# The down projection of a two-layer decoder: from plain tiles to one level of Strassen with left factors kept in DRAM

## The chip, the cores and the metric

One core of one Trainium2 chip runs the whole program. The metric is device time in microseconds; each kernel is run several times and the median is taken. The engines are named as in the profile: PE (TensorE matmul), PEld (its weight load), DVE (VectorE), ACT (ScalarE), POOL (GpSimd), SP (SyncE, which here only issues DMAs).

## The reference

Two layers, sequence length S = 1024, model width D = 1024, all fp32. Each layer is a mixer block (four kinds of mixer side by side, then an output projection), a layer norm, a gated feed-forward part of width 2816, and a second layer norm:

```
for l in range(DEPTH):
    h = mixer_block(x, w_in[l], ...)
    x = layer_norm(ALPHA * x + h, ln1_g[l], ln1_b[l])
    f = swiglu(x, w_gate[l], w_up[l], w_down[l])
    x = layer_norm(ALPHA * x + f, ln2_g[l], ln2_b[l])

def swiglu(x, w_gate, w_up, w_down):
    g = jnp.einsum('bsd,df->bsf', x, w_gate)
    u = jnp.einsum('bsd,df->bsf', x, w_up)
    return jnp.einsum('bsf,fd->bsd', jax.nn.silu(g) * u, w_down)
```

## The kernel before, in words

Every large matmul runs in fp32r as three matmuls: an operand is split into a high part (ACT, `split` L234) and a low part (DVE, or POOL where asked, L235), and hi·hi, hi·lo and lo·hi are added in one PSUM bank.

The feed-forward part has two stages for each layer. **f1** (gate and up) walks over i = 0..21, 22 tiles of 128 hidden units. For each i it does one level of Strassen: seven products of 12 matmuls each, 128x512 wide (`prod`), 84 matmuls an i. The right factors B11, T1 and so on of each i are formed by DVE and split into a ring of 12 tiles `wb`; the left factors (A11, S1 and so on, of the layer's input) were split once and stay in `RA`. DVE adds the products up in pieces of the big fp32 tile `FA`; p1, sg, v and w of an i are such pieces, and two sets alternate (`f1_tmp(i % 2)`). `f1_out` leaves the hidden values of the first 512 tokens in v and of the other 512 in w, and POOL writes both to DRAM (`hid`, L1229 and L1230). The last i has its own order of products (`f1_last`).

**f2** (down) is a plain product: 22 tiles of hidden units by 8 tiles of 128 tokens by two halves of the output by three, 1056 matmuls of 128x512 a layer. It goes over the 22 tiles in three chunks (8, 8, 6). A chunk's weights are loaded whole (512 KB a tile) and split into `RA` or `wy`; for each token tile the hidden values come back from `hid` (L1283), are split into a tile `h` on ACT and DVE, and two banks are added to the token's x in `FA` (L1330). In the first chunk x comes from DRAM (L1308) and POOL multiplies and shifts it by ln1 (L1311, L1312). After the last chunk come the layer norm, and in the first layer the transposes for the next (`make_T`).

Each engine takes its instructions in one fixed order, set when the program is built; instructions inside `high_priority` are drawn forward by a number of places (`w_ahead`). DMAs are issued by SP for loads and mostly by POOL for stores.

SBUF is laid out by pools: `RA` (all fp32r data that live long) first, `FA` behind it, and behind that the tiles of the stage: `wx` and `e` of the output projection, `wb` of f1, `wy` and `h` of f2. `FA` has 12168 words in each partition, 48672 bytes, which is 95 x 512 + 32; all other tiles are multiples of 512 bytes. So in the kernel before every stage tile starts 32 bytes off the 512-byte grid on which `RA` stands.

Of the kernel before, what the change touches and what calls it, by code (L numbers as in the profile page):

```python
# [9 lines left out]
F32 = mybir.dt.float32  # L10
# [38 lines left out]
F_SIZE = C_G1 + 16  # L49
# [91 lines left out]
class Trunk:  # L141
    def __init__(self, tc, t, scr):
        self.tc, self.nc, self.t, self.scr = tc, tc.nc, t, scr
        self.wring = [0, 1, 2]
        self.wpos = 0
        self.rpos = 0
        self.mmp = 0
# [943 lines left out]
    def form(self, tt):  # L1091
# [6 lines left out]
              (self.xt(1), self.xt(5)), (self.xt(0), self.xt(4)))[p]  # L1098
# [28 lines left out]
        S1 = self.xt((4, 5, 2, 3)[p])[:, 0:512]  # L1127
# [33 lines left out]
    def f1_prep(self, l, i):  # L1161
# [3 lines left out]
        T1, T2, T3, T4 = (self.f(FX + 2048 + j * 512, 512) for j in range(4))  # L1165
# [58 lines left out]
    def f1_out(self, i):  # L1224
        nc = self.nc
        p1, sg, v, w = self.f1_tmp(i)
        nc.scalar.activation(w, w, AF.Silu)
        nc.vector.tensor_tensor(w, w, p1, ALU.mult)
        nc.gpsimd.dma_start(self.scr["h"][i, 0], v)  # L1229
        nc.gpsimd.dma_start(self.scr["h"][i, 1], w)  # L1230
        del self.blk[i]

    def f1_last(self, i):
# [8 lines left out]
        tt_(p1, w, bank, ALU.add)  # L1242
        bank = self.prod(i, "A11", "B11")
# [23 lines left out]

    def f2(self, l):
        nc, t = self.nc, self.t
        lng, lnb = self.LNP[:, 0:1024], self.LNP[:, 1024:2048]  # L1270
        last = len(CHUNKS) - 1
        bp = hp = 0

        def load_h(tt, f0, nf):
            nonlocal hp
            raw = self.f(F_RAW + (self.rpos % NRAW) * 1024, nf * 128)
            self.rpos += 1
            H = self.H[hp % 3]
            hp += 1
            hh, hl = H[:, 0:nf * 128], H[:, 1024:1024 + nf * 128]  # L1280
            with self.tc.high_priority(offset=self.w_ahead):
                src = self.scr["h"][f0:f0 + nf, tt // 4, :, (tt % 4) * 128:(tt % 4) * 128 + 128]
                nc.sync.dma_start(raw.rearrange("p (f n) -> p f n", f=nf), src.rearrange("f p n -> p f n"))  # L1283
                self.split(hh, hl, raw)
            return hh, hl

        for ci, (f0, nf) in enumerate(CHUNKS):
            self.wring, self.wpos = DOWN_SLOTS[ci], 0
            units = []
            pre = {}  # L1290
            for i in range(nf):
                units.append(self.wload(t["w_down"][l, f0 + i]))
                if ci == 0 and i < 3:
                    pre[i] = load_h(i, f0, nf)
            if ci != 1:
                g, b = (t["ln1_g"], t["ln1_b"]) if ci == 0 else (t["ln2_g"], t["ln2_b"])
                nc.sync.dma_start(lng, g[l].partition_broadcast(128))
                nc.sync.dma_start(lnb, b[l].partition_broadcast(128))
                if ci == 0:
                    self.copy(lng, lng, scale=ALPHA)  # L1300
                    self.copy(lnb, lnb, scale=ALPHA)
            groups = [(0, 1, 2)] + [(i,) for i in range(3, 8)] if ci == 0 else [(i,) for i in range(8)]
            for group in groups:
                hs = [pre[tt] if tt in pre else load_h(tt, f0, nf) for tt in group]
                if ci == 0:
                    with self.tc.high_priority(offset=self.w_ahead):
                        for tt in group:
                            nc.sync.dma_start(self.xt(tt), self.scr["x1"][tt * 128:(tt + 1) * 128, :])  # L1308
                    for tt in group:
                        x = self.xt(tt)  # L1310
                        nc.gpsimd.tensor_tensor(x, x, lng, ALU.mult)  # L1311
                        nc.gpsimd.tensor_tensor(x, x, lnb, ALU.add)  # L1312
                banks = [self.B[(0, 1, 2, 3, 6, 7)[(bp + i) % 6]] for i in range(2 * len(group))]
                bp += len(banks)
                order = [(i, (ch,)) for ch in range(2) for i in range(nf)] if ci == last and group == (7,) \
                    else [(i, (0, 1)) for i in range(nf)]
                for i, chs in order:
                    for q, (hh, hl) in enumerate(hs):
                        hi, lo = hh[:, i * 128:(i + 1) * 128], hl[:, i * 128:(i + 1) * 128]
                        for ch in chs:  # L1320
                            wh, wl = (w[:, ch * 512:(ch + 1) * 512] for w in units[i])
                            bank = banks[2 * q + ch]
                            self.mm(bank, hi, wh, i == 0, False)
                            self.mm(bank, hi, wl, False, False)
                            self.mm(bank, lo, wh, False, i == nf - 1)
                for q, tt in enumerate(group):
                    x = self.xt(tt)
                    for ch in range(2):
                        xc = x[:, ch * 512:(ch + 1) * 512]
                        nc.vector.tensor_tensor(xc, xc, banks[2 * q + ch], ALU.add)  # L1330
                    if ci == last:
                        if l == L - 1:
                            rows = t["out"][tt * 128:(tt + 1) * 128, :]
                            self.layer_norm(x, lng, lnb, lambda c, xc: nc.sync.dma_start(
                                rows[:, c * 512:(c + 1) * 512], xc))
                        else:
                            self.layer_norm(x, lng, lnb)
                            nc.gpsimd.dma_start(self.scr["x2"][tt * 128:(tt + 1) * 128, :], x)
                            self.make_T(tt, x)
# [109 lines left out]
    def run(self):  # L1449
# [3 lines left out]
        nc.vector.memset(self.f(C_MH, 1), -0.5)  # L1453
        for l in range(L):
# [12 lines left out]
            with tc.tile_pool(name=f"f2_{l}", bufs=1, reuse_waits="tile") as pool:  # L1467
# [4 lines left out]
def trunk_kernel(tc, t, ext=None):  # L1472
    with tc.tile_pool(name="sb", bufs=1) as pool, \
            tc.tile_pool(name="ps", bufs=1, space=bass.MemoryType.PSUM) as psum, \
# [5 lines left out]
            "h": dram.tile([NFT, 2, 128, 512], F32, name="hid"),  # L1480
# [7 lines left out]
        k.setup(pool, psum)  # L1488
# [98 lines left out]
```

## Time and profile before

| | before |
|---|---|
| median of 3 runs | 2600.79 us (2598.32 to 2601.14) |
| profiled execution, own time | 2604.73 us |
| its span, first to last instruction | 2603.0 us |
| mean granted TensorE clock | 0.987 |
| f1 of layer 1, of layer 2 | about 606 to 1053.9, about 1894 to 2342 us |
| f2 of layer 1, of layer 2 | 1053.7 to about 1308, 2342 to 2603 us |

The times in the profile are those of one execution, some 4 us above the median. The granted clock is a share of TensorE's full speed. "Idle before" an instruction is time in which its engine had nothing to run, put down to what released it.

### The profile page before, as it was taken

How to read it: one execution, taken by the hardware profiler on the slowest of the kernel's cores; microseconds unless marked ns; L12 is line 12 of the kernel's file. 1: busy time of each engine (PE TensorE's matmuls, PEld its weight loads, DVE VectorE, ACT ScalarE, POOL GpSimd, SP SyncE). 2: the span in 40 equal slices, each digit the busy share in tenths (PEclk: the TensorE clock that was granted, in tenths of full speed). 3: DMA queues.
4: the chain of work that ended last, by engine and by line, in shares of the span. 5: the costliest groups of instructions: out<-in, count | busy, mean ns of one | idle time of the engine just before them, and what ended most of it. 6: DMA issues, size and time to landing. Idle time of an engine off the chain costs nothing. (4 is left out here: it accounts for less than half of the span.)

```text
span 2603.0 us, 36989 instructions
## 1 busy us (share of the span) xinstructions
PE 2519.5 (97%) x14128; PEld 2110.5 (81%) x14128; DVE 1606.5 (62%) x3267; ACT 1004.7 (39%) x1934; POOL 489.2 (19%) x498
## 2 busy tenths in 40 slices
PE   8999998998999999999999999989989999999998
PEld 8988887786888888788899988877768888887886
DVE  4775356668766665632757753566797666656336
ACT  4776552235333332221246765521453333322110
POOL 2214131124000000700222231301230000007002
PEclk9999999998999999999999999999989999999999
DMA  4112123213222223532321120142222222235222
GB/s 159 51 39 71 35 64 114 90 50 110 98 80 85 74 81 100 168 119 69 118 76 53 48 65 28 62 137 66 81 97 97 76 81 87 73 106 191 83 85 77
DMA packets 120673, 224.24 MB, mean 86 GB/s; under 512 B 16816, under 2 KB 67888, under 8 KB 120496
## 3 DMA queue, kind: packets, MB, share of 16 engines
q1 hardware_dynamic: 107792, 179.93, 21.9%
q0 software_dynamic: 12704, 41.95, 4.3%
q8 instruction: 111, 1.82, 0.3%
q14 instruction: 66, 0.54, 0.1%
HBM read 167.77 MB, written 46.20 MB: 82 GB/s over the span
## 5 line engine op out<-in xcount | busy, mean ns | idle before, releaser
L222 PE MATMUL bank<-RA,wb 128*128 128x512 f32 x3600 | 846.0, 397 | 10.4 <-ACT wb L234 7.4
L222 PE MATMUL bank<-RA 128*128 128x256 f32 (+6 forms) x5016 | 819.7, 314 | 14.3 <-ACT XA L229 10.2
L222 PEld LDWEIGHTS bank<-RA,wb 128*128 128x128 f32 x3600 | 679.5, 189 | 176.8 <-ACT wb L234 8.3
L222 PEld LDWEIGHTS bank<-RA 128*128 128x128 f32 (+1 forms) x5016 | 691.6, 192 | 76.9 <-issue 22.6
L222 PE MATMUL bank<-RA,h 128*128 128x512 f32 x1728 | 412.8, 396 | 6.2 <-DVE RA L235 5.5
L222 PEld LDWEIGHTS bank<-RA,h 128*128 128x128 f32 x1728 | 323.3, 188 | 86.8 <-DVE RA L235 7.3
L234 ACT ACTIVATE wb<-FA 128x512 fp32r<-128x512 f32 x300 | 188.5, 633 | 499.5 <-PE bank L222 479.5
L235 DVE TENSOR_TENSOR wb<-FA,wb 128x512 fp32r<-128x512 f32 x300 | 208.3, 699 | 5.6 <-ACT wb L234 3.4
L256 POOL TENSOR_TENSOR RA<-FA,RA 128x512 fp32r<-128x512 f32 (+2 forms) x112 | 144.1, 1306 | 320.9 <-ACT RA L255 296.9
L522 ACT ACTIVATE XA<-XA,FA 128x128 f32<-128x128 f32 (+3 forms) x192 | 148.5, 774 | 44.7 <-DVE FA L517 42.8
L517 DVE CUSTOM_DVE_ANT_0 XA<-bank,XA 128x384 f32<-128x384 f32 (+2 forms) x192 | 109.6, 571 | 75.8 <-PE bank L222 73.9
L235 DVE TENSOR_TENSOR RA<-FA,RA 128x1024 fp32r<-128x1024 f32 (+2 forms) x64 | 94.4, 1491 | 95.1 <-ACT RA L234 94.1
L1229 POOL DMA_DIRECT2D hid<-FA x44 | 23.9, 542 | 671.5 <-DVE FA L1220 640.1
L1330 DVE TENSOR_TENSOR FA<-FA,bank 128x512 f32<-128x512 f32 x96 | 64.2, 684 | 133.2 <-PE bank L222 133.2
L234 ACT ACTIVATE RA<-FA 128x512 fp32r<-128x512 f32 (+2 forms) x96 | 78.3, 826 | 169.0 <-DMA FA<-in_w_down 119.4
L225 PE MATMUL bank<-FA,XA 128*128 128x128 f32 (+1 forms) x824 | 127.0, 275 | 8.8 <-DMA XA<-mixed 5.2
L229 ACT ACTIVATE XA<-bank 128x512 f32<-128x512 f32 (+5 forms) x228 | 104.0, 483 | 55.7 <-PE bank L225 43.7
L225 PEld LDWEIGHTS bank<-FA,XA 128*128 128x128 f32 (+1 forms) x824 | 97.5, 141 | 21.7 <-DMA XA<-mixed 5.9
L234 ACT ACTIVATE h<-FA 128x1024 fp32r<-128x1024 f32 (+1 forms) x48 | 46.7, 988 | 170.8 <-PE bank L222 142.2
L280 POOL TENSOR_SCALAR FA<-FA 128x1 f32<-128x1 f32 (+1 forms) x48 | 17.7, 368 | 505.3 <-DVE FA L984 350.7
L222 PE MATMUL bank<-XA 128*64 128x128 f32 (+1 forms) x836 | 93.9, 294 | 7.9 <-ACT XA L229 4.7
L222 PE MATMUL bank<-wx,RA 128*128 128x512 f32 x384 | 99.7, 412 | 0.0
(190 smaller groups left out, 2679.4 us busy)
## 6 DMA issues: line engine op xcount, KB each, us to landing
FA<-in_w_in SPq DMA_DIRECT2D x44, 512.0 KB, 3.6
FA<-in_w_gate SPq DMA_DIRECT2D x44, 512.0 KB, 3.6
FA<-in_w_up SPq DMA_DIRECT2D x44, 512.0 KB, 3.3
hid<-FA POOLq DMA_DIRECT2D x88, 256.0 KB, 2.3
FA<-in_w_down SPq DMA_DIRECT2D x44, 512.0 KB, 3.4
FA<-hid SPq DMA_DIRECT2D x32, 512.0 KB, 4.0
x<-FA POOLq DMA_DIRECT2D x24, 512.0 KB, 3.0
FA<-x SPq DMA_DIRECT2D x24, 512.0 KB, 4.0
```

Source lines behind the costliest of these rows:

```text
L222: self.nc.tensor.matmul(out, lhsT=lhsT, rhs=rhs, start=start, stop=stop)
L225: self.nc.tensor.transpose(out, src, self.FA[0:p, C_ID:C_ID + p])
L229: self.nc.scalar.activation(out, src, AF.Copy)
L234: self.nc.scalar.activation(hi, src, AF.Copy)
L235: (self.nc.gpsimd if pool else self.nc.vector).tensor_tensor(lo, src, hi.bitcast(F32), ALU.subtract)
L256: nc.gpsimd.tensor_tensor(lo[:, c], raw[:, c], hi[:, c].bitcast(F32), ALU.subtract)
L280: nc.gpsimd.tensor_scalar(out, var, EPS, 1.0, ALU.add, ALU.mult)
L517: nc.vector.tensor_tensor_reduce(sv[m][:, c0:c0 + wd], bank[:, 0:wd], mask[:, off:off + wd], -scale, init, ALU.add, ALU.min, acc)
L522: self.last_exp = nc.scalar.activation(sv[m][:, 0:n], sv[m][:, 0:n], AF.Exp, bias=nb[:, m:m + 1], scale=-1.0, accum_out=den[:, m:m + 1])
L1229: nc.gpsimd.dma_start(self.scr["h"][i, 0], v)
L1330: nc.vector.tensor_tensor(xc, xc, banks[2 * q + ch], ALU.add)
```

## The change

The down projection becomes one level of Strassen, as f1 already is. Output, hidden values and w_down are cut in two along each axis; seven phases (`DOWN`) each multiply one left factor by one right factor. A phase has four units (token tiles of 128 out of 512), a unit 11 steps j by three matmuls of 128x512 into one bank: 7 x 4 x 33 = 924 matmuls a layer where there were 1056. Each unit's bank is added by DVE to between one and four half rows of x.

- The left factors are made and split while f1 runs. After every second i (`f1_left`), POOL forms S1 to S4 by four additions. For each of the seven factors, `left_put` splits it into one of three tiles `st` (high part on ACT, low part on POOL), and POOL writes the tile, 512 KB, to DRAM in pieces of 1 KB. In f2 each unit loads its ready-made pair of parts, 1.44 MB in three pieces, into six tiles `h`.
- w_down is loaded in half-width blocks (256 KB) and stays raw in SBUF; DVE forms T1 to T4 in place; each phase splits 11 blocks (ACT high, DVE low).
- All loads of f2 are chained on SP in program order (`in_order`).
- The SBUF layout: `FA` goes to the right end, `RA` becomes `RB` and two tiles `RT` (which turn into raw weights `RW` in f2), and every fp32r tile now starts at the same place modulo 512 bytes.
- `f1_last` takes its products in another order, with A11 and A12 last.

The core of the diff:

```diff
@@ F_SIZE
-F_SIZE = C_G1 + 16
+F_SIZE = C_G1 + 16 + 80
+DOWN = [("A12", "B21"), ("S4", "B22"), ("A11", "B11"), ("S1", "T1"), ("S3", "T3"), ("S2", "T2"), ("A22", "T4")]
...
@@ f1_out
-        nc.gpsimd.dma_start(self.scr["h"][i, 0], v)
-        nc.gpsimd.dma_start(self.scr["h"][i, 1], w)
         del self.blk[i]
+        self.f1_left(i)
+
+    def left_put(self, j, name, src):
+        st = self.ST[self.lfp % 3].rearrange("p (t h n) -> p t h n", t=4, h=2)
+        self.lfp += 1
+        self.split(st[:, :, 0, :], st[:, :, 1, :], src.rearrange("p (t n) -> p t n", t=4), True)
+        self.nc.gpsimd.dma_start(self.scr["s" + name][:, :, j, :].rearrange("t p n -> p t n"),
+                                 st.rearrange("p t h n -> p t (h n)").bitcast(F32))
+
+    def f1_left(self, i):
+        tt_ = self.nc.gpsimd.tensor_tensor
...
+        if i % 2 == 0:
+            self.left_put(j, "A12", vb)
+            self.left_put(j, "A22", wb)
+            return
...
+        tt_(S1, wa, wb, ALU.add)
+        tt_(S2, S1, va, ALU.subtract)
+        tt_(S4, vb, S2, ALU.subtract)
+        tt_(S3, va, wa, ALU.subtract)
+        self.left_put(j, "A11", va)
+        self.left_put(j, "S4", S4)
+        self.left_put(j, "S1", S1)
+        self.left_put(j, "S3", S3)
+        self.left_put(j, "S2", S2)
...
@@ f2
+        self.in_order(nc.sync.dma_start(lng, t["ln1_g"][l].partition_broadcast(128)))
+        self.in_order(nc.sync.dma_start(lnb, t["ln1_b"][l].partition_broadcast(128)))
+        self.copy(lng, lng, scale=ALPHA)
+        self.copy(lnb, lnb, scale=ALPHA)
+        for j in range(NPR):
+            self.down_load(l, j, "B21")
+            self.down_put(0, j)
...
+                    self.mm(bank, hh, wh, j == 0, False)
+                    self.mm(bank, hh, wl, False, False)
+                    self.mm(bank, hl, wh, False, j == NPR - 1)
```

ACT at the passage from f1 to f2 in the first layer, before. `h` are the split hidden values of the first three token tiles, L1227 and L1249 the last activations of f1, `RA` the first down weights:

```order
L229 ACTIVATE FA_71<-bank1_73 128x512
L229 ACTIVATE FA_71<-bank4_76 128x512
L1249 ACTIVATE FA_71<-FA_71 128x512
L234 ACTIVATE h0_8292<-FA_71 128x1024
L234 ACTIVATE h1_8293<-FA_71 128x1024
L234 ACTIVATE h2_8294<-FA_71 128x1024
L1227 ACTIVATE FA_71<-FA_71 128x512
```

The same place now. L1254 and L1306 are the last activations of f1, the `st` rows are the high parts of A11, S1, S4, S3 and S2 of the last pair (in this order), L258 the scaling of ln1, and `RB` and behind it the first down weights:

```order
L1254 ACTIVATE FA_80<-FA_80 128x512
L1306 ACTIVATE FA_80<-FA_80 128x512
L261 ACTIVATE st0_5764<-FA_80 128x4x128
L261 ACTIVATE st2_5766<-FA_80 128x4x128
L261 ACTIVATE st1_5765<-FA_80 128x4x128
L261 ACTIVATE st0_5764<-FA_80 128x4x128
L261 ACTIVATE st1_5765<-FA_80 128x4x128
L258 ACTIVATE lnp0_8546<-lnp0_8546 128x1024
L258 ACTIVATE lnp1_8547<-lnp1_8547 128x1024
L261 ACTIVATE RB_79<-FA_80 128x512 x6
```

Before, the first splits of f2 stood ahead of the last activation of f1; now seven instructions stand between the last activation of f1 and the first split of f2, and the fourth and fifth of the five `st` rows write a tile that an earlier one of them filled.

POOL at the same place, before (L1229 and L1230 are the stores of hidden values, L1311 and L1312 x by ln1):

```order
L1230 DMA hid_66<-FA_71 128x512
L1229 DMA hid_66<-FA_71 128x512
L1311 TENSOR_TENSOR FA_71<-FA_71,LNP_8291 128x1024 x6
L1230 DMA hid_66<-FA_71 128x512
L1312 TENSOR_TENSOR FA_71<-FA_71,LNP_8291 128x1024 x2
L1311 TENSOR_TENSOR FA_71<-FA_71,LNP_8291 128x1024
```

And now: L1278, L1281, L1279 and L1280 are S1, S3, S2 and S4 of the last pair, L262 low parts, L1264 stores of left factors, L1372 and L1373 x by ln1:

```order
L1278 TENSOR_TENSOR FA_80<-FA_80 128x512
L1281 TENSOR_TENSOR FA_80<-FA_80 128x512
L1279 TENSOR_TENSOR FA_80<-FA_80 128x512
L262 TENSOR_TENSOR st0_5764<-FA_80,st0_5764 128x4x128
L262 TENSOR_TENSOR st2_5766<-FA_80,st2_5766 128x4x128
L1280 TENSOR_TENSOR FA_80<-FA_80 128x512
L1264 DMA leftA11_71<-st0_5764 128x4x256
L1264 DMA leftS1_72<-st2_5766 128x4x256
L262 TENSOR_TENSOR st1_5765<-FA_80,st1_5765 128x4x128
L1264 DMA leftS4_70<-st1_5765 128x4x256
L262 TENSOR_TENSOR st0_5764<-FA_80,st0_5764 128x4x128
L1264 DMA leftS3_73<-st0_5764 128x4x256
```

Before the x rows POOL now has four additions, five low parts and five stores of the last pair, and the stores of A11 and S4 stand behind S4's addition.

## Rows read from the trace of the kernel before

**Rows 1.** The page's part 1: engine, busy time, share of the span, instructions.

```profile
PE 2519.5 (97%) x14128; PEld 2110.5 (81%) x14128; DVE 1606.5 (62%) x3267; ACT 1004.7 (39%) x1934; POOL 489.2 (19%) x498
```

**Rows 2.** Groups of PE's instructions, shapes apart: busy, mean ns, idle before.

```profile
L222 PE MATMUL bank<-RA,wb 128*128 128x512 f32 x3600 | 846.0, 397 | 10.4 <-ACT wb L234 7.4 <-POOL RA L235 3.0
...
L222 PE MATMUL bank<-RA,h 128*128 128x512 f32 x1728 | 412.8, 396 | 6.2 <-DVE RA L235 5.5 <-DVE h L235 0.5
```

**Rows 3.** Busy time by window: PE, PEld, DVE, ACT, POOL, PEclk, DMA share, GB/s.

```profile
740.00:1040.00 300.00, 300.00 (x1288) 241.50 (x1287) 190.61 (x297) 93.43 (x150) 17.00 (x32) 1.00 0.25 84
1054.00:1062.00 8.00, 7.95 (x35) 6.11 (x34) 4.90 (x6) 3.82 (x4) 2.68 (x2) 1.00 0.89 339
...
0.00:20.00 20.00, 12.60 (x63) 11.52 (x64) 4.11 (x7) 6.83 (x11) 5.52 (x10) 1.00 0.86 305
590.00:630.00 40.00, 31.38 (x139) 24.52 (x137) 33.33 (x58) 25.21 (x46) 20.81 (x22) 0.90 0.18 71
```

**Rows 4.** Timeline of PE: start, length from first to last, one unbroken series each.

```profile
899.72 22.56 PE L222 MATMUL bank<-RA,wb 128*128 128x512 f32 x96
...
1236.76 5.76 PE L222 MATMUL bank<-RA,h 128*128 128x512 f32 x24
1242.36 2.91 PE L222 MATMUL bank<-wy,h 128*128 128x512 f32 x12
...
1689.24 16.41 PE L222 MATMUL bank<-RA 128*128 128x512 f32 x71
```

**Rows 5.** Timeline of the passage from f1 to f2 in layer 1.

```profile
1049.58 2.95 ACT L234 ACTIVATE h<-FA 128x1024 fp32r<-128x1024 f32 x3
...
1053.72 10.27 PE L222 MATMUL bank<-RA,h 128*128 128x512 f32 x42
...
1053.92 0.69 DVE L1252 TENSOR_TENSOR FA<-FA,bank 128x512 f32<-128x512 f32 x1 [1.32 <-PE bank L222]
...
1058.12 2.26 ACT L231 ACTIVATE LNP<-LNP 128x1024 f32<-128x1024 f32 x2 [2.85 <-DMA LNP<-in_ln_g]
...
1059.32 18.11 POOL L1311 TENSOR_TENSOR FA<-FA,LNP 128x1024 f32<-128x1024 f32 x6 [5.88 <-issue]
...
1061.71 16.79 DVE L235 TENSOR_TENSOR RA<-FA,RA 128x1024 fp32r<-128x1024 f32 x5 [3.10 <-ACT RA L234]
...
1065.22 8.43 PE L222 MATMUL bank<-RA,h 128*128 128x512 f32 x35 [1.23 <-DVE RA L235]
```

**Rows 6.** Single lines: durations in ns, least, median and most.

```profile
L235 POOL TENSOR_TENSOR RA<-FA,RA x32: 1282/1602/2800, 573.4 to 1922.1; 128x512 fp32r<-128x512 f32 x32
...
L1311 POOL TENSOR_TENSOR FA<-FA,LNP x16: 2389/3368/3398, 1059.3 to 2386.4; 128x1024 f32<-128x1024 f32 x16
...
L1071 POOL DMA_DIRECT2D x<-FA x16: 590/606/624, 567.0 to 1908.3; - x16
```

**Rows 7.** DMA issues: count, size each, median us from issue to landing.

```profile
hid<-FA POOLq DMA_DIRECT2D x88, 256.0 KB, 2.3
...
x<-FA POOLq DMA_DIRECT2D x24, 512.0 KB, 3.0
...
mixed<-FA POOLq DMA_DIRECT2D x2, 1024.0 KB, 12.7
```

**Rows 8.** Timeline of PE around its longest wait ahead of f1.

```profile
605.73 1.12 PE L225 MATMUL bank<-FA 128*128 128x128 f32 x4 [3.84 <-ACT FA L1070]
...
606.50 4.19 PE L222 MATMUL bank<-wx,RA 128*128 128x512 f32 x9
...
611.19 1.90 PE L222 MATMUL bank<-wx,RA 128*128 128x512 f32 x6
```

**Rows 9.** Timeline inside f1 (DVE and ACT while PE runs on).

```profile
908.14 0.63 ACT L234 ACTIVATE wb<-FA 128x512 fp32r<-128x512 f32 x1 [2.17 <-PE bank L222]
...
911.12 0.69 DVE L1217 TENSOR_TENSOR FA<-FA,bank 128x512 f32<-128x512 f32 x1 [1.51 <-PE bank L222]
911.72 0.68 DVE L1218 TENSOR_TENSOR FA<-FA,bank 128x512 f32<-128x512 f32 x1
```

More of the change, by code (lines that the diff above doesn't have):

```diff
@@ L178, in open_f1 @@
         self.WB = [pool.tile([128, 1024], F32R, name=f"wb{i}") for i in range(12)]
+        self.ST = [pool.tile([128, 1024], F32R, name=f"st{i}") for i in range(3)]
     def open_f2(self, pool):
-        self.WX = [pool.tile([128, 2048], F32R, name=f"wy{i}") for i in range(2)]
-        self.LNP = pool.tile([128, 2048], F32, name="LNP")
-        self.H = [pool.tile([128, 2048], F32R, name=f"h{i}") for i in range(3)]
+        tiles = {}
+        for name, dt in F2_TILES:
+            tiles[name] = pool.tile([128, 1024], dt, name=name)
+        self.DW = [tiles[f"dw{i}"] for i in range(4)]
+        self.H = [tiles[f"h{i}"] for i in range(6)]
+        self.LNP = [tiles[f"lnp{i}"] for i in range(2)]
+        self.WD = [tiles[f"wd{i}"] for i in range(3)]
     def r(self, off, n, p0=0, p1=128):
-        return self.RA[p0:p1, off:off + n]
+        if off >= R_W:
+            return self.RB[p0:p1, off - R_W:off - R_W + n]
+        return self.RT[off // 8192][p0:p1, off % 8192:off % 8192 + n]
     def f(self, off, n, p0=0, p1=128):
@@ L1265, in f1, with down_raw, in_order @@
                 self.f1_last(i)
+    def down_raw(self, j):
+        B21 = self.f(F_RAW + j * 512, 512) if j < 6 else self.WD[(j - 6) // 2][:, (j % 2) * 512:(j % 2) * 512 + 512]
+        B12, B22 = (self.RW[i][:, j * 512:(j + 1) * 512] for i in (1, 0))
+        B11 = self.WD[2][:, 512:1024] if j == 10 else self.RW[j // 5][:, 5632 + (j % 5) * 512:6144 + (j % 5) * 512]
+        return dict(B11=B11, T1=B11, T2=B22, T4=B21, B12=B12, T3=B12, B21=B21, B22=B22)
+    def in_order(self, ins):
+        if self.sp_last is not None:
+            self.behind(ins, self.sp_last)
+        self.sp_last = ins
@@ new lines, in down_slot, with down_put, down_left @@
+    def down_slot(self, ph, j):
+        n = DOWN_SLOTS[ph][j]
+        w = self.r(R_W + n * 1024, 1024) if n < 12 else self.DW[n - 12]
+        return w[:, 0:512], w[:, 512:1024]
+    def down_put(self, ph, j):
+        self.split(*self.down_slot(ph, j), self.down_raw(j)[DOWN[ph][1]])
+    def down_left(self, ph, tt, p):
+        j0, j1 = PIECES[p]
+        n = self.hp
+        self.hp += 1
+        h = self.H[n % 6]
+        h = h[:, 0:(j1 - j0) * 256]
+        with self.tc.high_priority(offset=self.w_ahead):
+            self.in_order(self.nc.sync.dma_start(h.bitcast(F32), self.scr["s" + DOWN[ph][0]][tt, :, j0:j1, :].rearrange("p j n -> p (j n)")))
+        return h.rearrange("p (j h n) -> p j h n", h=2, n=128)
@@ new lines, in down_x, with down_done @@
+    def down_x(self, l, tt):
+        nc = self.nc
+        x = self.xt(tt)
+        with self.tc.high_priority(offset=self.w_ahead):
+            self.in_order(nc.sync.dma_start(x, self.scr["x1"][tt * 128:(tt + 1) * 128, :]))
+        nc.gpsimd.tensor_tensor(x, x, self.LNP[0], ALU.mult)
+        nc.gpsimd.tensor_tensor(x, x, self.LNP[1], ALU.add)
+    def down_done(self, l, tt):
+        nc, t = self.nc, self.t
+        x = self.xt(tt)
+        lng, lnb = self.LNP
+        if l == L - 1:
+            rows = t["out"][tt * 128:(tt + 1) * 128, :]
+            self.layer_norm(x, lng, lnb, lambda c, xc: nc.sync.dma_start(rows[:, c * 512:(c + 1) * 512], xc))
+        else:
+            self.layer_norm(x, lng, lnb)
+            nc.gpsimd.dma_start(self.scr["x2"][tt * 128:(tt + 1) * 128, :], x)
+            self.make_T(tt, x)
@@ L1268, in f2 @@
     def f2(self, l):
         nc, t = self.nc, self.t
[L1270 to L1339, printed above, removed]
@@ new lines, in f2, with left @@
+        self.hp = 0
+        units = [(ph, tt) for ph in range(7) for tt in ((0, 2, 3, 1) if ph < 5 else range(4))]
+        lefts = {}
+        def left(u):
+            if u < len(units):
+                lefts[u] = [self.down_left(*units[u], p) for p in range(3)]
+        left(0)
+        for u, (ph, tt) in enumerate(units):
+            q = u % 4
+            if (ph, q) == (3, 0):
+                self.in_order(nc.sync.dma_start(lng, t["ln2_g"][l].partition_broadcast(128)))
+                self.in_order(nc.sync.dma_start(lnb, t["ln2_b"][l].partition_broadcast(128)))
+            left(u + 1)
+            name = {0: "B22", 1: "B11", 2: "B12"}.get(u // 3)
+            if name:
+                for j in range(4 * (u % 3), min(4 * (u % 3) + 4, NPR)):
+                    self.down_load(l, j, name)
+            for t_ in {0: [0], 1: [2], 2: [3, 1], 3: [4], 4: [6], 5: [7, 5]}.get(u, []):
+                self.down_x(l, t_)
+            early, late = ([], []) if ph == 6 else (range(EARLY), range(EARLY, NPR))
+            nxt = DOWN[min(ph + 1, 6)][1]
+            if q == 2:
+                for js in (early, late):
+                    for j in js:
+                        if nxt != "T4":
+                            self.down_add(nxt, j)
+                        if js is early:
+                            self.down_put(ph + 1, j)
+                if nxt == "T2":
+                    for j in range(NPR):
+                        self.down_add("T4", j)
+            if (ph, q) == (5, 0):
+                self.rt.release()
+                if l < L - 1:
+                    self.open_rt()
+            bank = self.B[(0, 1, 2, 3, 6, 7)[u % 6]]
+            H = lefts.pop(u)
+            for p, (j0, j1) in enumerate(PIECES):
+                for j in range(j0, j1):
+                    hh, hl = H[p][:, j - j0, 0, :], H[p][:, j - j0, 1, :]
+                    wh, wl = self.down_slot(ph, j)
+                    self.mm(bank, hh, wh, j == 0, False)
+                    self.mm(bank, hh, wl, False, False)
+                    self.mm(bank, hl, wh, False, j == NPR - 1)
+                    if q == 3 and j in late:
+                        self.down_put(ph + 1, j)
+            lo, hi = self.xt(tt), self.xt(tt + 4)
+            both = lambda x: x.rearrange("p (c n) -> p c n", c=2)
+            for x in ((lo[:, 0:512],), (lo[:, 512:1024],), (both(lo), both(hi)), (lo[:, 512:1024], hi[:, 512:1024]),
+                      (both(hi),), (lo[:, 512:1024], both(hi)), (hi[:, 0:512],))[ph]:
+                tt_(x, x, bank if len(x.shape) == 2 else bank.unsqueeze(1).to_broadcast([128, 2, 512]), ALU.add)
+            if ph == 5:
+                self.down_done(l, tt)
+            elif ph == 6:
+                self.down_done(l, tt + 4)
@@ L1466, in run @@
                 self.f1(l)
-            with tc.tile_pool(name=f"f2_{l}", bufs=1, reuse_waits="tile") as pool:
+            with tc.tile_pool(name=f"f2_{l}", bufs=1, reuse_waits="tile", side="right") as pool:
                 self.open_f2(pool)
@@ L1479, in trunk_kernel @@
             "x2": dram.tile([S, D], F32, name="x2"),
-            "h": dram.tile([NFT, 2, 128, 512], F32, name="hid"),
+            **{f"s{n}": dram.tile([4, 128, NPR, 256], F32, name=f"left{n}") for n, _ in DOWN},
             "negm": dram.tile([32, 128], F32, name="negm"),
```

58 lines of the change are left out of this document (46 added, 12 removed).

## The prediction

> **What bounds the kernel now.** I read the page's busy times first: PE is busy for 97% of the span [rows 1], so the time is the number of matmuls by what each takes, plus some 80 us of waits. Next the groups of PE's instructions: in f1 and f2 it waited 10.4 and 6.2 us in all [rows 2], and inside f1 it ran a window of 300 us without a gap [rows 3]. There DVE was busy 190.61 of 300 us and ACT 93.43, and both waited for PE to give a tile or a bank free [rows 9]. So in both stages the bound is the rate at which PE takes matmuls, and the other engines matter where they stop feeding it.
>
> The rate itself is in the timeline of PE. A series of n matmuls lasts n-1 steps and one whole matmul, whose mean is about 0.40 us [rows 2]. The f1 series gives (22.56 - 0.40) / 95 = 233.3 ns a step, the f2 series with weights from RA (5.76 - 0.40) / 23 = 233.0; but wy by h gives (2.91 - 0.40) / 11 = 228.2 and RA by RA (16.41 - 0.40) / 70 = 228.7 [rows 4]. The slow series pair RA with a tile behind FA, so 32 bytes off its 512-byte grid; the fast ones pair tiles on one grid. The gap is about 4.8 ns.
>
> **What is removed.** 1056 - 924 = 132 matmuls a layer, 264 in all. At 233.3 ns: -61.6 us. The 6.2 us of waits in the old f2 go too, as their causes, weight splits by DVE that POOL held up, are written anew: -6.2 us.
>
> **All tiles on one grid.** f1 has 22 x 84 = 1848 matmuls a layer, the new f2 924: 5544 in all, which now read two operands on the same grid. If the offset is what makes the 4.8 ns: -26.6 us. Bounds: 0, if something else that wy by h and RA by RA share makes them faster, and this value. I take the full one, since four series fall into two groups by the offset alone. [...]
>
> **The passage from f1 to f2.** Before, the three h splits ran at 1049.58, ahead of the end of f1, and PE went over at 1053.72 without a wait [rows 5]. Now ACT has five st splits and two lnp scalings ahead of the first weight split, in fixed order, and two of the five wait for stores from the tile they overwrite. Let t = 0 be PE's last matmul of f1. An addition on POOL takes 1.28 us at least, taken as 1.29 [rows 6], its issue of a store 0.6 to 0.8, as 0.606 is shown for a store of whole rows [rows 6] and these have more pieces. A DVE step after PE, a Silu and a product make wa ready at 1.5 and va at 2.4, by the spacing of like steps [rows 5, 9]. POOL: S1 until 2.9, S3 4.2, S2 5.5, the low parts of A11 and S1 8.1, S4 9.4, the stores of A11 10.2 and S1 10.9, S4's low part 12.2 and its store 12.9. A store lands 2.3 to 3.0 us after its issue for hid and x [rows 7], or up to 6.3, half of the 12.7 of the 1 MB store of mixed [rows 7]. So A11's tile comes free at about 13, S4's at 15.5 to 19, then ACT splits S2 (0.63), scales ln1 twice (2.26 [rows 5]), splits the first weight block (0.63), and DVE its low part (0.69): PE starts at about 20, or 23 with slow stores. I take 21. Then POOL runs its x rows, and beside such rows five DVE splits of 1024 took 16.79 us while POOL had 18.11 for six [rows 5]. DVE's 11 low parts of phase 0 fall into that: 2 us more. Per layer 23, together **+46 us**. The bounds: the loads of lnp, 11 weight blocks and the first left piece, 4.4 MB, wait for f1's last tiles and at 339 GB/s [rows 3] take 13 us from the product before the last, so PE waits at least 10 us whatever ACT does; above, 27.
>
> **The clock behind that wait.** After a wait of 3.84 us, nine matmuls took 4.19 us where 0.40 + 8 x 0.233 = 2.27 are usual, and the next six 1.90 for 1.57 [rows 8]; that window's granted clock is 0.90 [rows 3]. I take 2.5 us a layer: **+5 us** (bounds 0 and, for a longer wait, 10).
>
> **Inside the new f2.** A unit is 33 x 228.5 ns = 7.54 us. The loads of the first six units are 1.44 MB of left factors, four blocks of 256 KB and about 0.7 MB of x each: 3.2 MB or 424 GB/s. The two busiest windows give 339 / 0.89 = 381 and 305 / 0.86 = 355 GB/s for full queues [rows 3]. At 370 six units need 52 us instead of 45, 7 late, against left factors issued a unit ahead and the stop at the passage. Before, no wait at all came from there. DVE makes up to 44 T additions in phases 1 to 3, in units that lie interleaved with their successors. I take **+3 us** in all (bounds 0 and 16).
>
> **Inside f1.** Each pair of i adds 4 additions and 7 low parts on POOL and 7 high parts on ACT (4.4 us in 38.4, hidden: ACT is a third busy). POOL: 11 x 1.29 + 7 x 0.7 = 19 us, hidden too, but DVE pays: POOL's rows and DVE's exclude each other where both read SBUF, as L1311 and L235 show [rows 5]. DVE has 190.61 / 300 x 39.2 = 24.9 us a pair, or 21.9 at the 0.60 us at which back-to-back rows start [rows 9]; with 11 x 1.29 = 14.2 that is 36.1 of 38.4. DVE also waits once a pair, when the next v is to be written, for S4's addition at 9.4 to 13 where it comes there at 8.4. The ring of 12 weight tiles covers three products, 8.2 us, as ACT fills a tile when PE leaves it [rows 9]. I take 0.4 us a pair: **+8 us** (bounds 0 and 90).
>
> **The sum.** -61.6 - 6.2 - 26.6 + 46 + 5 + 3 + 8 = -32.4 us. The profiled execution took 2604.73; it would take 2572.3, and since its median is 3.9 below, I predict 2568.4.
>
> **The rivals.** A difference under 0.2%, 5.2 us, can't be told from none here.
>
> - *Short passage.* The stores land fast and ACT's chain is overlapped, so that only the loads hold PE, for 10 us: 2 x (23 - 11) = 24 us less, **2544**. For it: nothing but the spread of POOL's durations. Against it: the order on ACT, which is fixed.
> - *The grid is worth nothing.* **2595**. For it: only two of the four series are fast, and both also pair tiles that are close together. Against it: h by RA and h by wy differ only in wy's place.
> - *f1 is bound by DVE and POOL.* If POOL's rows take 1.6 us, the median of its splits [rows 6], 11 are 17.6; with DVE's 21.9 to 24.9 that is 39.5 to 42.5 us for a pair against 38.4, so 1.1 to 4.1 us more each; over 22 pairs 24 to 90 us in place of my 8. From 1.9 us a pair on, the kernel is slower than before. At 3 us: 2568 + 58 = **2626**. For it: the exclusion [rows 5], and DVE's order, which queues weight splits behind the blocked v. Against it: eight of DVE's rows for an i read one operand from PSUM (as L1217 [rows 9]), POOL's shortest is 1.29, and its chain lies in half of the pair. [...]
>
> **How the numbers follow.** My forecast 0.52, the short passage 0.12, no gain from the grid 0.18, f1 bound 0.18. The likeliest case's own range is 2552 to 2584. To leave out 2 in 10 the whole range goes from 2540 to 2608: it keeps the short passage and the grid at nothing, and cuts off most of f1 bound. Faster by over 0.2%: 0.51 + 0.12 + 0.10 + 0.03 = 0.76; within 0.2%: 0.01 + 0.06 + 0.03 = 0.10; slower: 0.02 + 0.12 = 0.14.
>
> **What would show it.** PE's matmul count falls by 264 (in the records, some may be missing). A series of f1 steps at 228 to 229 ns if the grid counts, at 233 if not. At the passage PE waits about 20 us, released by DVE's low part of the first `RB` block, with ACT idle on stores of st before it; the granted clock falls in the window behind. In f1, PE's idle sum stays under 10 us a layer; in f2 the waits for h or RB stay under 2 us a layer. The prediction is wrong if f1's PE shows waits for wb in every pair, if the passage takes under 15 or over 27 us, or if f2's units wait for DMA of left factors.

## The result, and the profile after

The changed kernel takes 2559.7 us (2557.58 to 2563.31, 4 runs) against 2600.89 for the kernel before on the same chip: a ratio of 0.984 (95% interval [0.982, 0.986]), 41 us faster. The forecast was 2568.4 us, 32.4 us less than before, with a range of 2540 to 2608. The profiled execution took 2563.31 us, its span is 2561.5 instead of 2603.0, its mean granted clock 0.976 instead of 0.987.

The page of the changed kernel, parts 1 and 5 (the groups of the two stages):

```profile
PE 2435.6 (95%) x13864; PEld 2067.6 (81%) x13864; DVE 1777.4 (69%) x3401; ACT 1078.4 (42%) x2150; POOL 899.8 (35%) x806
...
L249 PE MATMUL bank<-RT,wb 128*128 128x512 f32 x2016 | 465.8, 389 | 0.0
...
L249 PE MATMUL bank<-RB,wb 128*128 128x512 f32 x1584 | 373.7, 394 | 10.4 <-ACT wb L261 7.1
...
L249 PE MATMUL bank<-RB,h 128*128 128x512 f32 x1272 | 309.2, 397 | 53.8 <-ACT RB L261 38.8
```

PE has exactly 264 matmuls fewer [rows 1]. f1 waits as much as before, 10.4 us [rows 2], though POOL has almost twice the work; f2 waits 53.8 us where the old one waited 6.2. The timeline of PE inside f1, one unbroken series to a row:

```profile
908.86 8.32 PE L249 MATMUL bank<-RB,wb 128*128 128x512 f32 x36
917.02 8.32 PE L249 MATMUL bank<-RT,wb 128*128 128x512 f32 x36
```

The second row starts 8.16 us behind the first, 36 matmuls later: 226.7 ns a step, against 233.3 [rows 4]. And the passage from f1 to f2:

```profile
1046.26 0.77 POOL L1264 DMA_DIRECT2D leftA<-st  x1
...
1049.74 0.63 ACT L261 ACTIVATE st<-FA 128x512 fp32r<-128x512 f32 x1 [2.77 <-DMA leftA<-st]
...
1053.16 0.63 ACT L261 ACTIVATE st<-FA 128x512 fp32r<-128x512 f32 x1 [2.79 <-DMA leftS<-st]
1053.70 1.99 ACT L258 ACTIVATE lnp<-lnp 128x1024 f32<-128x1024 f32 x2
...
1055.59 3.21 ACT L261 ACTIVATE RB<-FA 128x512 fp32r<-128x512 f32 x6
...
1056.26 0.80 PE L249 MATMUL bank<-RB,h 128*128 128x512 f32 x1 [19.39 <-ACT RB L261]
1056.34 2.37 POOL L1372 TENSOR_TENSOR FA<-FA,lnp 128x1024 f32<-128x1024 f32 x1
...
1059.33 1.65 PE L249 MATMUL bank<-RB,h 128*128 128x512 f32 x3 [2.27 <-DVE RB L262]
...
1062.11 28.11 PE L249 MATMUL bank<-RB,h 128*128 128x512 f32 x116 [1.13 <-DVE RB L262]
```

Read from the bottom: PE waits 19.39 us for the first split of `RB`; ACT makes that split behind the two scalings of ln1, these behind the last st split, and the last two st splits wait for stores from their tiles. Before, PE went over without a wait [rows 5]. Behind the first low parts stand two more waits while POOL multiplies x.

A third place was not there before, in unit 4 of f2 (units counted from 0; it is the first of phase 1). The timeline of DVE and of POOL there, then PE's own waits of 1090 to 1110 us (us in total, how many, the longest):

```profile
1090.24 13.89 DVE L262 TENSOR_TENSOR RB<-RW,RB 128x512 fp32r<-128x512 f32 x6 [4.70 <-ACT RB L261]
```

```profile
1091.78 5.67 POOL L1373 TENSOR_TENSOR FA<-FA,lnp 128x1024 f32<-128x1024 f32 x2
1097.40 2.81 POOL L1372 TENSOR_TENSOR FA<-FA,lnp 128x1024 f32<-128x1024 f32 x1
1100.29 2.69 POOL L1373 TENSOR_TENSOR FA<-FA,lnp 128x1024 f32<-128x1024 f32 x1
```

```profile
PE bank L249 <- DVE RB L262: 3.6, 2, 1.8
```

Six low parts, 0.68 us each where nothing runs beside them, took 13.89 us: five of them ended only behind a row of POOL. The windows of the changed kernel (columns as in [rows 3]) show the clock fall behind both places where PE had waited, to 0.53 and 0.64 of full speed in the mean (0.50 from 1056 to 1064 us and from 1104 to 1108):

```profile
1056.00:1066.00 10.00, 6.34 (x15) 4.20 (x16) 9.77 (x9) 7.48 (x15) 5.40 (x3) 0.53 0.15 52
...
1104.00:1112.00 8.00, 8.00 (x24) 6.25 (x24) 8.00 (x8) 0.00 (x0) 5.07 (x2) 0.64 0.66 189
```

To set a sum against the forecast's I added, over each stage of both traces, what every step of a 128x512 matmul took beyond the usual 226.7 or 233.3 ns; that counts waits and slow clock together. f1 is taken from its first product with a tile `wb` on, and steps between which PE had other work are left out:

| us, both layers | forecast | measured |
|---|---|---|
| 264 matmuls fewer, at 233.3 ns | -61.6 | -61.6 |
| the grid, 5544 matmuls | -26.6 | -37.0 (6.67 ns each) |
| passage, waits and clock | +51 | +53.0 (26.2 and 26.8) |
| the rest of f2, new less old (16.4 less 7.3) | -3.2 | +9.1 |
| f1, new less old (11.3 less 8.7) | +8 | +2.6 |
| everything else | 0 | -7.6 (the remainder) |
| sum | -32.4 | -41.5 (span) |

### The profile page after: what moved, and what is told of

Read it like the earlier page. It is cut to its first block, busy times and chain, and to the rows that moved or that the text cites. A ratio compares the mean times of both kernels' runs of the same rounds, so it can differ in the third digit from the quotient of the medians.

```text
span 2561.5 us, 37438 instructions
## 1 busy us (share of the span) xinstructions
PE 2435.6 (95%) x13864; PEld 2067.6 (81%) x13864; DVE 1777.4 (69%) x3401; ACT 1078.4 (42%) x2150; POOL 899.8 (35%) x806
## 4 chain that ended last, share of the span: by engine, by line
PE 85%; DVE 6%; DMA 4%; issue 2%; ACT 2%; POOL 1%; SPq 0%; DVEq 0%; POOLq 0%; ACTq 0%
PE bank L249 80%; PE bank L252 5%; DMA FA<-in_w_out 2%; DVE RB L262 1%; DVE FA L1141 0%; DMA FA<-in_w_gate 0%; DVE XA L728 0%; DMA XA<-mixed 0%; ACT XA L256 0%; DVE FA L1157 0%; DVE FA L1156 0%; DMA FA<-in_w_in 0%; POOL st L262 0%; DMA leftS<-st 0%; ACT XA L549 0%
## 5 line engine op out<-in xcount | busy, mean ns | idle before, releaser
L249 PE MATMUL bank<-RB,RT 128*128 128x256 f32 (+2 forms) x4224 | 668.6, 302 | 8.9 <-ACT XA L256 8.1
L249 PEld LDWEIGHTS bank<-RB,RT 128*128 128x128 f32 x4224 | 578.4, 193 | 48.6 <-issue 18.8
L249 PE MATMUL bank<-RT,wb 128*128 128x512 f32 x2016 | 465.8, 389 | 0.0
L249 PEld LDWEIGHTS bank<-RT,wb 128*128 128x128 f32 x2016 | 378.9, 188 | 79.0 <-ACT RT L261 0.3
L249 PE MATMUL bank<-RB,wb 128*128 128x512 f32 x1584 | 373.7, 394 | 10.4 <-ACT wb L261 7.1
L249 PEld LDWEIGHTS bank<-RB,wb 128*128 128x128 f32 x1584 | 300.8, 190 | 75.8 <-ACT wb L261 7.9
L249 PE MATMUL bank<-RB,h 128*128 128x512 f32 x1272 | 309.2, 397 | 53.8 <-ACT RB L261 38.8
L262 POOL TENSOR_TENSOR st<-FA,st 128x512 fp32r<-128x512 f32 x154 | 224.1, 1462 | 317.6 <-ACT st L261 317.1
L249 PEld LDWEIGHTS bank<-RB,h 128*128 128x128 f32 x1272 | 242.5, 192 | 109.7 <-ACT RB L261 39.6
L262 DVE TENSOR_TENSOR wb<-FA,wb 128x512 fp32r<-128x512 f32 x300 | 285.9, 956 | 12.6 <-ACT wb L261 12.0
L283 POOL TENSOR_TENSOR RB<-FA,RB 128x512 fp32r<-128x512 f32 (+2 forms) x112 | 144.4, 1310 | 311.4 <-ACT RB L282 287.7
L1456 DVE TENSOR_TENSOR FA<-FA,bank 128x512 f32<-128x512 f32 (+1 forms) x80 | 69.8, 896 | 107.0 <-PE bank L249 100.1
```

The costliest lines, as they stand in the source:

```text
L249: self.nc.tensor.matmul(out, lhsT=lhsT, rhs=rhs, start=start, stop=stop)
L262: (self.nc.gpsimd if pool else self.nc.vector).tensor_tensor(lo, src, hi.bitcast(F32), ALU.subtract)
L283: nc.gpsimd.tensor_tensor(lo[:, c], raw[:, c], hi[:, c].bitcast(F32), ALU.subtract)
L1456: tt_(x, x, bank if len(x.shape) == 2 else bank.unsqueeze(1).to_broadcast([128, 2, 512]), ALU.add)
```

## The experiments

Medians of the kernel before differ by a few us between chips, so only ratios to it, from the same chip, are compared; 0.001 is 2.6 us. The changed kernel stands at 0.984.

**The grid taken back, and the grid alone.** The first kernel shifts the stage tiles of the changed one:

```diff
-F_SIZE = C_G1 + 16 + 80
+F_SIZE = C_G1 + 16
...
     def open_f1(self, pool):
+        self.pad = pool.tile([128, 8], F32, name="pad")
```

> The changed kernel with the tiles off the grid: FA loses its 80 words of padding, so the tiles of f2 (h and dw) start 320 bytes off RB modulo 512 but on one grid among themselves, and a pad of 32 bytes ahead of wb puts the ring of f1 32 bytes off RT and RB. Theory (the offset between the two operands makes the step): f1 steps go from 227 to about 233 ns, RB by h to about 233, dw by h stays at 227; 3696 and 1272 matmuls times 6.7 ns are 33 us more than the changed kernel, about 2593. Rival (the step has another cause, such as the kind or the region of the tiles): steps stay at 227 and the time at 2560.

The second gives only the grid to the kernel before (and the smaller DMA scratch that makes room for it, which the change has too):

```diff
-F_SIZE = C_G1 + 16
+F_SIZE = C_G1 + 16 + 120
...
-    nc = bacc.Bacc("TRN2", target_bir_lowering=False, num_devices=1)
+    nc = bacc.Bacc("TRN2", target_bir_lowering=False, num_devices=1, dynamic_dma_scratch_size=4096)
```

> The kernel before with the grid alone: FA is padded by 120 words, so that every fp32r tile starts at the same place modulo 512, and nothing else changes. Theory: f1 steps, RA by h and wx by RA fall from 233.3 to 226.7 ns; (3600 + 96 + 1728 + 384) x 6.7 ns = 39 us less than before, about 2562, as fast as the whole change. Rival (the faster steps of the changed kernel come from the new f2 or its tiles and not from the offset): no change, 2601.

Without the grid: 0.9958 [0.9944, 0.9973], 30 us slower than the changed kernel (33 expected), so that all the rest of the change is worth some 11 us. With the grid alone: 0.9876 [0.9854, 0.9899], 32 us faster than before. Here 39 were expected; the steps fell in full, and what took the other 7 us was not looked for. Series of PE, of the kernel without the grid (the last two rows are f2) and of the grid alone:

```profile
917.25 8.56 PE L250 MATMUL bank<-RB,wb 128*128 128x512 f32 x36
...
1224.35 5.06 PE L250 MATMUL bank<-RB,h 128*128 128x512 f32 x21
1229.25 2.90 PE L250 MATMUL bank<-dw,h 128*128 128x512 f32 x12
```

```profile
898.62 31.67 PE L222 MATMUL bank<-RA,wb 128*128 128x512 f32 x139
```

Taking 0.40 us off for the last matmul: 233.1 ns for RB by wb, 233.0 for RB by h, 227.3 for dw by h, whose tiles stay on one grid; and 226.6 for RA by wb on the grid. In the same stage, by the same instructions, only pairs with unequal offsets are slow. The rival is out: the offset makes the step. That the scratch does not is shown by the second of the next two runs, which keeps the old one and is as fast.

**Which offsets.** The kernel before with other paddings of FA (+8 and +56 words), one run each:

> The kernel before with FA longer by 8 words, so that the stage tiles start 64 bytes off RA modulo 512 in place of 32. If only equal places modulo 512 are fast, f1 steps stay at 233 ns; if places equal modulo 64 are enough, they fall to 227.

> The kernel before with FA longer by 56 words, so that the stage tiles start 256 bytes off RA modulo 512. If only equal places modulo 512 are fast, f1 steps stay at 233 ns; if equal places modulo 256 are enough, they fall to 227.

```profile
898.83 31.43 PE L222 MATMUL bank<-RA,wb 128*128 128x512 f32 x134
```

```profile
898.71 31.67 PE L222 MATMUL bank<-RA,wb 128*128 128x512 f32 x139
```

Off by 64 bytes a step takes 233.3 ns; off by 256, 226.6. So of the offsets modulo 512 that were run, 32, 64 and 320 bytes are slow (233.0 to 233.3 ns), and 0 and 256 are fast (226.6 or 226.7, and 227.3 for dw by h): the 512 of the change is more than was needed here. Whether 128 would do was not tried. The single times were 2614.6 and 2577.5 us; runs of the kernel before lay between 2593 and 2612 on those chips, so the steps are the evidence, not these. Each of the two times contains one wait of PE of nearly 12 us in f2 of layer 2, for a DVE low part that elsewhere takes 1.22 us. Off by 256 bytes, PE's wait and that low part:

```profile
PE bank L222 <- DVE RA L235: 13.5, 2, 11.8
```

```profile
2333.65 17.77 DVE L235 TENSOR_TENSOR RA<-FA,RA 128x1024 fp32r<-128x1024 f32 x1 [2.37 <-ACT RA L234]
```

The last section comes back to such rows.

**Another order at the passage.** The tiles st live beside FA, and three of the four tiles `dw` for weights of f2 are now these same tiles. Dependencies that only fix the order on an engine (NoSync) put ACT's last left factors, and the scaling of ln1, behind the last high part of phase 0 (`self.hi`):

```diff
-        self.f1_left(i)
+        if i < NFT - 1:
+            self.f1_left(i)
...
         for j in range(NPR):
             self.down_load(l, j, "B21")
             self.down_put(0, j)
+        self.ahead = self.hi
+        self.f1_left(NFT - 1)
...
+        if self.ahead:
+            self.behind(self.hi, self.ahead)
```

> The changed kernel with another order on ACT at the passage: the tiles st live beside FA, the eleven splits of phase 0 stand ahead of the last pair's left factors on ACT, and those and the scaling of ln1 stand behind them. Same work. Theory (PE waits 19.4 us a layer for ACT's chain of st tiles and nothing else): the wait falls to about 3 us with up to 4 more while POOL's additions hold up DVE's first low parts, and the slow clock behind it goes; 2 x (26.4 - 7) = 39 us less than the changed kernel, about 2521, between 2512 and 2536. Rival (the loads of lnp, weights and left factors hold PE for at least 10 us, as the prediction's lower bound has it): 2 x 13 = 26 us less or fewer, 2534 to 2550.

0.9791 [0.9774, 0.9809]: 13 us less than the changed kernel, a third of what was expected, and by the number the rival's case. PE's waits at the passage of layer 1 and DVE's and POOL's timeline there:

```profile
PE bank L249 <- DVE RB L262: 11.6, 5, 8.5
PE bank L249 <- ACT RB L261: 2.0, 1, 2.0
```

```profile
1046.47 13.10 DVE L262 TENSOR_TENSOR RB<-wd,RB 128x512 fp32r<-128x512 f32 x5
```

```profile
1048.40 1.50 POOL L1267 DMA_DIRECT2D leftS<-st  x2
1049.91 2.35 POOL L1376 TENSOR_TENSOR FA<-FA,lnp 128x1024 f32<-128x1024 f32 x1
1052.22 1.26 POOL L262 TENSOR_TENSOR st<-FA,st 128x512 fp32r<-128x512 f32 x1
1053.44 2.34 POOL L1377 TENSOR_TENSOR FA<-FA,lnp 128x1024 f32<-128x1024 f32 x1
```

ACT's wait fell from 19.4 to 2.0 us, so its order was the cause. The loads, which by the prediction hold PE for at least 10 us, do not: PE has no wait for a DMA here, so the rival's number came without its cause. But DVE's low parts of phase 0 now meet POOL's chain, and PE waits for them. The longest of its waits, 8.5 us, is for a single low part that lasted 9.6 us, from 1048.77 on.

**No x rows, and x rows on DVE.** The first leaves out x's multiplication and shift by ln1, the second moves it:

```diff
-        nc.gpsimd.tensor_tensor(x, x, self.LNP[0], ALU.mult)
-        nc.gpsimd.tensor_tensor(x, x, self.LNP[1], ALU.add)
+        nc.vector.tensor_tensor(x, x, self.LNP[0], ALU.mult)
+        nc.vector.tensor_tensor(x, x, self.LNP[1], ALU.add)
```

> The changed kernel without POOL's multiplication and shift of x by ln1 in f2 (so x is added as it was loaded). Theory (these rows hold up DVE's low parts, which makes the short waits behind the first unit and the three waits around 1098 to 1104 us with their slow clock): 2 x (3.4 + 7.6) = 22 us less than the changed kernel, about 2538. Rival (the waits around 1098 come from late loads of raw weights): only the 3.4 us a layer go, about 2553, and PE still waits there, with DVE waiting for ACT and ACT for DMA.

> The changed kernel with x's multiplication and shift by ln1 on DVE in place of POOL, nothing else. Theory (DVE loses more to POOL's rows, which it waits out at 2.4 to 2.9 us each, than it would need to do them itself at 1.2 us, and it is idle most of the time between 1066 and 1090 us): nearly as fast as without these rows, 18 to 23 us less than the changed kernel, a ratio of 0.975 to 0.978 to the kernel before; the waits at 1098 to 1104 us go. Rival (16 more rows of 1.2 us make DVE late for the T additions and splits, or hold it up while x is loaded): less than 10 us gained, new waits for DVE in phases 1 to 3.

0.9763 [0.9744, 0.9782] and 0.9746 [0.9717, 0.9776]: 21 and 25 us less than the changed kernel (22, and 18 to 23, were expected). In both, PE has one wait in the whole f2 of layer 1 (the rows of the second, and DVE's x rows):

```profile
PE bank L249 <- ACT RB L261: 19.4, 1, 19.4
```

```profile
L1372 DVE TENSOR_TENSOR FA<-FA,lnp x16: 1217/1224/1227, 1064.6 to 2368.7; 128x1024 f32<-128x1024 f32 x16
```

The waits around 1098 us, and the two short ones behind the first unit's start, came from POOL's rows alone; late loads of raw weights do not show. DVE does such a row itself in 1.22 us, where one of its low parts lasted up to 3.0 us in place of 0.68 beside each row of POOL.

**Both edits, and three tries at the rest.**

> The kernel with the first splits ahead on ACT, and x's rows on DVE as well. Theory (what took back two thirds of the first order's gain is that DVE's low parts of phase 0 stand against POOL's rows; without the x rows nine rows of the last pair's left factors are left there): per layer some 10 us of waits and 2 of slow clock at the passage in place of 26.4, and no waits around 1098; 2 x (13 to 15 + 7.6) = 41 to 45 us less than the changed kernel, a ratio of 0.967 to 0.969. Rival (the last pair's chain holds DVE whatever else POOL has to do): as much as the two edits gave apart, 13 + 20, a ratio of 0.972.

0.9659 [0.9624, 0.9695], 48 us less than the changed kernel (41 to 45 were expected) and 89 less than before, both by the ratios. PE's waits of layer 1 from the passage on:

```profile
PE bank L249 <- DVE RB L262: 3.1, 4, 1.4
PE bank L249 <- ACT RB L261: 2.0, 1, 2.0
PE bank L249 <- DMA h<-leftS: 0.5, 2, 0.3
```

To free DVE of POOL's remaining rows, the additions S1 and S3 of the last pair (`first`, `third`) were made to wait for phase 0's last low part (`held`):

```diff
+        for ins in (first, third) if self.ahead else ():
+            self.tc.add_manual_dep(ins.ins, self.held.ins.name, mybir.DependencyInfo(mybir.DependencyClass.Sync, mybir.DependencyReason.DATA), reason="later")
```

> The kernel with both edits, and POOL's additions for the last pair made to wait for DVE's last low part of phase 0. Theory (only the exclusion between POOL and DVE is left at the passage): PE waits about 3 us there and runs the first unit unhindered, 2 x (22 + 7.6) = 59 us less than the changed kernel, a ratio of 0.960 to 0.963. Rival (the later chain makes the stores of S4 and S2 late, so that phase 1 waits for its left factors or for weights split into the tiles st): 5 to 15 us a layer come back, a ratio of 0.966 or more.

Then the token tiles of every phase, and the loads of x, in the order 0, 1, 2, 3 (`{0: [0], 1: [1], 2: [2, 3], ...}` for `{0: [0], 1: [2], 2: [3, 1], ...}`), and then S1 to S4 of the last pair in x tiles 3 and 4, with one tile of x loaded a unit (`2: [2], 3: [3], ...`):

> The kernel of the later chain, with the token tiles of every phase in the order 0, 1, 2, 3 and x loaded in that order, so that the x tiles which lie where POOL keeps S1 to S4 are asked for one unit later. Theory (SP, in fixed order, stood behind the load of x tile 2, which waited for POOL's last low part, and held up the left factors of unit 3): the wait of 5.7 us a layer for h and the slow clock behind it go, 2 x 8 = 16 us less than the later chain, a ratio of 0.960 to 0.963. Rival (the left factors are late because the stores are): no change to the later chain, 0.967.

> The kernel before this one with POOL's S1 to S4 of the last pair kept where x tiles 3 and 4 will lie in place of 2 and 3, and x loaded one tile a unit, so that no load of x ahead of unit 4's left factors waits for POOL. Theory (the wait of 5.4 us for h, moved from unit 3 to unit 4, is still SP standing behind x loads that wait for POOL's last low part): that wait and the 2 us of slow clock behind it go, 2 x 7.5 = 15 us less, a ratio of 0.960 to 0.963. Rival (unit 4's left factors come late for another reason, such as the stores of S4 or full queues): no change, 0.967.

They came to 0.9675 [0.9648, 0.9703], 0.9672 [0.9653, 0.9691] and 0.9675 [0.9649, 0.9701]: none is faster than the two edits alone, and all three expectations of 0.960 to 0.963 missed. PE's longest wait in f2 of layer 1, in that order:

```profile
PE bank L249 <- DMA h<-leftA: 5.7, 1, 5.7
```

```profile
PE bank L249 <- DMA h<-leftS: 5.4, 1, 5.4
```

```profile
PE bank L249 <- ACT st L261: 5.5, 1, 5.5
```

DVE was free each time (0.3 us of waits for it), and each time some 5.5 us came back elsewhere. First it was the left factors of unit 3: SP issued them behind a load of x, and that at 1062.67, when POOL's last low part ended at 1062.65. Then it was those of unit 4, in the same way (1064.79 and 1064.77). At last it was the weights of phase 1: the split that PE waited for stands on ACT behind four others, and these waited for raw weights:

```profile
1075.17 2.64 ACT L261 ACTIVATE RB<-RW 128x512 fp32r<-128x512 f32 x4 [2.94 <-DMA RW<-in_w_down]
```

The queues moved 406 GB/s in that stretch, and these loads took 8.7 us to land. In the second layer the same split waited for a store from its tile st, and PE for 3.6 us. The later chain is late for whatever comes next.

**How near f1 is to its bound.**

```diff
+        for _ in range(2):
-        tt_(S1, wa, wb, ALU.add)
+            tt_(S1, wa, wb, ALU.add)
...
```

> The changed kernel with POOL's four additions of each pair of i done twice, with the same results. Theory (f1 had slack: the ring of weight tiles covers what POOL takes from DVE): inside f1 PE's waits grow by under 3 us a layer, and at the passage the last pair's chain is 4 to 5 us longer: 8 to 14 us more than the changed kernel, a ratio of 0.987 to 0.990. Rival (f1 stood just at the bound, as the prediction's third rival has it): 5 us more in most of the 22 pairs, 60 us or more, a ratio over 1.005.

1.0021 [1.0007, 1.0034], 46 us more than the changed kernel; both expectations missed, the first by far. DVE's longest wait inside f1 of the changed kernel, then of this one PE's wait and DVE's low parts (layer 1):

```profile
DVE FA L1241 <- POOL FA L1280: 23.1, 9, 3.7
```

```profile
PE bank L249 <- DVE FA L1241: 12.5, 7, 3.1
```

```profile
L262 DVE TENSOR_TENSOR wb<-FA,wb 128x512 fp32r<-128x512 f32 x102 | 111.9, 1102 | 22.0 <-ACT wb L261 19.6 <-PE bank L249 2.4
```

The changed kernel's DVE already waits for S4 in 9 of the 11 pairs of layer 1, 2.6 us in the mean, without PE feeling it. Four more rows on POOL (in the changed kernel 1.25 us at least, with medians of 1.29 to 1.75), 5 to 6.4 us a pair, stretched DVE's low parts from 948 to 1102 ns in the mean and cost PE about 2 us in 7 of the 11 pairs, and the clock in some (18 us more in f1 of layer 1, by the same sum of steps), and 8 us at its passage.

## Why the prediction held, point by point

**Removed matmuls:** as predicted, to the last one.

**The grid:** the cause was right, its size was off: 6.67 ns a step, not 4.8, so -37.0 for -26.6, beyond the bound that I had set. The fast series from which I took 228.2 and 228.7 were short or not clean: of the eleven steps of wy by h at 1242.36, which follow slow ones, the first five still take 228 to 236 ns, the other six 226 or 227. With nothing but the tiles' offsets changed, the step went from 226.7 to 233.1 ns in the changed kernel, and from 233.3 to 226.6 in the kernel before (the +56 words). The rival of a worthless grid is out.

**The passage:** right in mechanism and size. Counted from the end of PE's last matmul of f1 (1056.26 - 19.39 = 1036.87), A11's tile came free at 12.9 us (forecast about 13), the split of S2 started at 16.3 (15.5 to 19), PE at 19.4 (about 20, taken as 21); the two waits behind it are 3.4 us (forecast 2), and with the clock the whole is 26.5 a layer against 25.5. One detail was wrong: what released PE was ACT's high part of the first block, for its first matmul needs no more; DVE's low part made the wait behind it. And one bound was wrong: the loads were issued from 1015 us on, long before the end of f1, so they would not have held PE for 10 us; the rival of a short passage rested on that.

**Inside f2:** the step that failed. I took 3 us and named loads and T additions; 16.4 us were there, just above my bound of 16, 8 in each layer, in units 4 and 5, and neither of the two was the cause. My sign for this term, waits for h or RB under 2 us a layer, failed too: 3.6 us in layer 1. The exclusion between POOL's x rows and DVE's splits, which I priced for phase 0, goes on as long as there are x rows, into the splits of phase 1. Moving the rows away took it to under 1 us.

**Inside f1:** 2.6 us for a forecast 8, so the term was too large, and the third rival did not come true. Its mechanism is there, though: DVE waits for S4 once a pair as worked out, and doubling the additions shows that the margin is less than the 5 to 6.4 us a pair that they take of POOL's time. So f1 was nearer to that bound than its small wait shows.

**The sum:** 10.4 us too little for the grid, 12.3 too good for f2, 5.4 too bad for f1, and 2 too good at the passage; these nearly cancel, and that the forecast came within 9 us is in that part luck. The remaining 7.6 us lie outside f1 and f2 as counted here: in layer 1, PE's first product with a tile `wb` started 6.4 us earlier (623.68 for 630.04). The grid gives a little of it, 480 matmuls of the output projection and of f1's first products at some 5 ns (a series of 57 with wx takes 13.09 us for 13.46, one of 18 with e 4.36 for 4.44). No run shows the rest to be the change's doing: in the kernel before with 64 bytes of offset, whose steps in f1 are as slow, that product starts almost as early, so most of it can be the spread between executions:

```profile
625.47 0.50 PE L222 MATMUL bank<-RA,wb 128*128 128x512 f32 x1 [3.68 <-ACT wb L234]
```

## What to carry to other kernels

Where a kernel is bound by matmuls at a constant step, compare steps between pairs of operand tiles: here a padding of 480 bytes alone gave 32 us, without any Strassen, and Strassen without the grid 11 of the 41. When a stage's last work is put on another engine's fixed queue, count what the next stage's first instruction stands behind; and before giving POOL two-input work, look at what DVE does at that moment: here DVE did in 1.22 us a row of x that took POOL 2.36 to 2.88. When a wait is taken away, look for the next in line: three edits each left a wait of some 5.5 us at another place.

## What the runs showed of the hardware that was not expected

- The step of a 128x512 matmul in fp32r was 226.6 to 227.3 ns in those series of the changed kernel and of the experiments whose operands start at the same place modulo 512 bytes or 256 off, and 233.0 to 233.3 where they are off by 32, 64 or 320 bytes. Why was not found, and 128 was not tried.
- POOL's x rows of 1024 and DVE's low parts, both with two operands in SBUF, excluded each other: low parts of 0.68 us lasted mostly 2.8 to 2.9 beside such rows (1092.30 to 1106 us of the changed kernel). A DVE row with one operand in PSUM was not held: L1456 took 0.68 us at 1106.83 while POOL's row of 1106.44 ran.
- The turns were not always fair. In the kernel with the first splits ahead, one DVE low part of 0.68 us lasted 9.6, across three rows of POOL, a store and another row that followed each other without a gap; elsewhere in the same trace the two engines alternate (six low parts in 9.12 us from 1037.43 on). In the two kernels before with other paddings a low part of 1.22 us lasted 14.7 and 17.8, and in f1 of layer 2 of the changed kernel one of 0.68 lasted 7.9. Each of these ended 0.5 to 1.1 us behind the last row of an unbroken run of POOL. What decides between the two patterns was not tried. The low parts of the first of these kernels (least, median and most, in ns):

```profile
L262 DVE TENSOR_TENSOR RB<-wd,RB x18: 677/681/9605, 1046.5 to 2503.1; 128x512 fp32r<-128x512 f32 x18
```
